# A hybrid decoder layer on one core: operand blocks fetched ahead, form sums on GpSimd, the norm chain in steps, and more Strassen units in FFN-out

## The chip, the cores and the metric

The kernel runs on one core of a Trainium2 chip. The core has TensorE (PE in the profile, its weight loads PEld), VectorE (DVE), ScalarE (ACT), GpSimd (POOL) and SyncE (SP, which only issues transfers); each takes its own instructions in order. The metric is the device time in microseconds of one execution, median of the runs.

## The reference

512 tokens, model width 2048, everything in float32. One layer:

```python
h = rmsnorm(x, attn_norm_g);  proj = h @ w_in        # u, v_sgu, q, k, v_att, g_a, g_b
y_a = u * chunked_spatial_gating(v_sgu);  y_b = stick_breaking_attention(q, k, v_att)
x = x + (sigmoid(g_a) * (y_a @ w_up_a) + sigmoid(g_b) * (y_b @ w_up_b)) @ w_o
h = rmsnorm(x, ffn_norm_g);  gate, up = split(h @ w_ffn_in)    # 2048 -> 2 x 5632
x = x + (silu(gate) * up) @ w_ffn_out                          # 5632 -> 2048
x = x + sigmoid(rmsnorm(x, ple_norm_g) @ w_ple_gate) * (p @ w_ple)
```

## The kernel before

Every product of float32 values is made of three matmuls (`mm3`): each operand is split into a high part (ScalarE's copy, L245 for activations and L313 for weights) and a low part (VectorE's subtraction, L246 and L310), and high x high, high x low and low x high are added up in PSUM. Activations lie transposed, 128 rows by 512 tokens.

The work is cut into **units**: 256 rows of the inner dimension against 256 columns of the output (an output **pair**). A unit is either plain ("P": four blocks of the weight, 12 matmuls of 512 columns) or one level of Strassen's scheme ("S": seven products of 128x128 blocks with half of the tokens, 21 matmuls of 256 columns; in FFN-in, where both output halves are doubled, L589 and L591). `OUT`, `PASSES` and `GATE` at the file's head say which unit of a stage is which. FFN-out has 22 units; their operands don't fit on the chip together, so it runs in three passes over the eight output pairs, of 8, 7 and 7 units, and the running sum goes to memory and back between passes (`sum`; pass 3 also reads `x1` and writes `x2`). The first pair of a stage (`j == 0`) is always computed plain.

An activation's operand is a **form**. Forms lie in the arena `parts`, 16 places (`PLACE`); a Strassen form takes two places of 1792 columns, a plain one 2048 columns. Raw blocks, weight landings and temporaries lie in the arena `wholes`. A form of a Strassen unit is built in steps: load the block (`load`, SP), scale by the norm's gain (`gained`, L451, where there is one), four sums of 128x256 (`plain_first`, L464, VectorE) and the split of the four plain blocks; a step later the split of three sums (128x3x256); last, once the plain pair has used it, the split of one more (128x256). `late_form` builds it for `x1` (FFN-in), `hid` (FFN-out) and `x2` (the gate), `x_form` for the input.

What sets the order: `tick()` is called two or more times in each double unit of a pair. A tick starts the first form of the queue `builds` if its source is there and the arenas have room, and runs the waiting steps of others. The schedule of each engine is then fixed when the program is built. Weights go through four landing blocks and three slots (`Weights`): SP brings a landing, and for a Strassen weight GpSimd issues a transfer that adds two blocks onto it (L317); ScalarE and VectorE split it into a slot (L313, L310), VectorE makes two sums of it (L329). `prepare_early` and `prepare_late` do this ahead of TensorE.

At the start, three output pairs of `p @ w_ple` (`ple_pair`) run while the first `x` blocks come in, then three pairs of the first projection share the plain forms of x (`w_first`). Five more ple pairs (two halves of output each, copied out by L766) stand between the out projection and FFN-in. `Norm` adds up squares (L831, L835); its chain is a matmul with ones (L844), a mean, a power on GpSimd (L852), and a spread of the result over the rows (L817, L819).

Of the kernel before, what the change touches and what calls it, by code (L numbers as in the profile page):

```python
# [63 lines left out]
def hybrid_layer(  # L64
# [44 lines left out]
    class Arena:  # L109
        def __init__(self, name, n, dt):  # L110
            self.tile, self.dt = keep.tile([P, n], dt, name=name), dt
            self.holes = [(0, n)]

        def take(self, n, how="low"):

            spots = []
            for start, size in self.holes:
                end = start + size
                if how == "place":
                    start = -(-start // PLACE) * PLACE  # L120
                if end - start >= n:
                    spots.append((-end, end - n) if how == "high" else (start, start))
# [7 lines left out]
        def give(self, block):  # L130
            holes = sorted(self.holes + [(block.start, block.n)])
# [54 lines left out]
    def tick():  # L186

        clock[0] += 1
        last, units = traced()[-1], dict(newest)
        if builds and builds[0].ready() and fits(builds[0].sizes):  # L190
            builds.popleft().step()
        while waiting and waiting[0][0] <= clock[0]:
            heapq.heappop(waiting)[2]()
        for i in reversed(traced()):
            if i is last:
                break
            if i.engine in units:
                tc.add_manual_dep(
                    i, units[i.engine],
                    mybir.DependencyInfo(mybir.DependencyClass.NoSync,  # L200
                                         mybir.DependencyReason.DATA),
                    reason="in its place among the units")

    class Staged:


        def __init__(self, steps):
            self.steps, self.result, self.done, self.at = steps, None, False, 0

        def advance(self):  # L210
            self.at += 1
            try:
                next(self.steps)
            except StopIteration as e:
                self.result, self.done = e.value, True

        def step(self):
            if not self.done:
                self.advance()
                if not self.done:  # L220
                    after(1, self.step)

        def get(self):
# [172 lines left out]
    def plain_weights(src):  # L396
        slot, w = Weights(src.rearrange("p (b c) -> p b c", b=4), 1, "P").get()
        return slot, w

    class Form(Staged):  # L400


        def __init__(self, kind, steps, sizes, ready):
            super().__init__(steps(self))
            self.kind, self.sizes, self.ready = kind, sizes, ready
            self.blocks, self.at_plain, self.used = None, kind == "P", False

        def get(self):
# [4 lines left out]
        def plain(self):  # L413

            if self.kind == "P":
                return self.get()
            while not self.at_plain:
                self.advance()
            return self.halves(self.operand())

# [9 lines left out]
        def use_plain(self):  # L430

            self.used = True
            if not self.done:
                after(1, self.step)

# [9 lines left out]
    def load(src, n=1024):  # L445
        b = take(n)
        nc.sync.dma_start(out=b.f(0, 1024), in_=src)
        return b
# [6 lines left out]
    def plain_first(form, raw):  # L455


        b, s, v = cut(raw.f()), take(768), take(256)
        t, x = cut(s.f()), form.operand()
        for out, p, q, op in ((t[:, 0], b[:, 1], b[:, 0], ALU.subtract),  # L460
                              (v.f(), b[:, 1], b[:, 3], ALU.subtract),
                              (t[:, 1], t[:, 0], b[:, 3], ALU.subtract),
                              (t[:, 2], t[:, 1], b[:, 2], ALU.add)):
            nc.vector.tensor_tensor(out=out, in0=p, in1=q, op=op)  # L464
# [12 lines left out]
    def late_form(src, ready=always, gain=None):  # L477


        def steps(form):  # L480
            w = src()
            form.blocks = (parts.take(2 * PLACE, "place"),)
            if gain:
# [5 lines left out]
        return Form("S", steps, [(parts, 2 * PLACE, "place")] + [(wholes, 1024, "low")] * 2, ready)  # L489

# [21 lines left out]

    def plain_form(src, ready=always, gain=None, raw=1024, how="low"):
        def steps(form):
            w = src()
            hi, lo = form.blocks = parts.take(1024, how), parts.take(1024, how)
            if gain:
                gained(hi.own(), w.f(), *gain)
# [7 lines left out]
            else:  # L526
# [5 lines left out]
        return Form("P", steps, [(parts, 1024, how)] * 2 + [(wholes, raw, "low")] * bool(raw),  # L532
                    ready)

# [212 lines left out]
    def ple_operands():  # L747
        raw = load(pT)
        hi, lo = parts.take(1024, "high"), parts.take(1024, "high")
        split_into(hi.own(), lo.own(), raw.f())  # L750
        give(raw)
        ps_p.extend((hi, lo))

    def ple_pair(j, planned=True):
        slot, ((wh, wl),) = next_weights() if planned else plain_weights(w_ple[j])
        if planned:
            prepare_early()
            prepare_late()
        o = wide()
        for i in range(2):  # L760
            ps = bank()
            for k in range(2):
                s = 2 * i + k
                xh, xl = (x.own(k * T, (k + 1) * T) for x in ps_p)
                mm3(ps, wh[:, s], wl[:, s], xh, xl, k == 0, k == 1)
            nc.scalar.activation(o[:, i * T : (i + 1) * T], ps, AF.Copy)  # L766
        d = tc.dram_tile([P, 1024], F32, name=nm("ple"))
# [13 lines left out]
    def load_x():  # L781
        x_raw.append(take(1024))
        nc.sync.dma_start(out=x_raw[-1].f(), in_=xT[len(x_raw) - 1])

    ple_operands()
    ple_pair(0, False)
    load_x()
# [36 lines left out]
    class Norm:  # L824
# [4 lines left out]
        def add(self, raw):  # L829
# [8 lines left out]
            if self.done == KU:  # L838
                self.chain = Staged(self.steps())

        def steps(self):
# [24 lines left out]
    def x_form(k):  # L866
        def steps(form):
            while len(x_raw) < min(k + 2, KU):
                load_x()
            form.blocks = (parts.take(2 * PLACE, "place"),)  # L870
            w = take(1024)
            gained(w.f(), x_raw[k].f(), g_attn, k)
# [225 lines left out]
    def made():  # L1098
# [3 lines left out]
        for i in range(1, 3):  # L1102
            ple_pair(i, False)
        ple_done()
        ps = [Pair("P" * KU) for _ in range(3)]
        for k in range(KU):
            for p, src in zip(ps, (w_first[i] for i in range(3))):
                slot, (w,) = plain_weights(src[:, k * 4 * P : (k + 1) * 4 * P])
                p.add("P", [w], [xs[k].plain()], False)
# [35 lines left out]
    def y_form(c, i):  # L1145
        return plain_form((lambda: y_a[i]) if c == "a" else lambda: load(y_spill[i]),
                          lambda: len(y_done) == 8, raw=0 if c == "a" else 1024)

# [70 lines left out]
    def spilled_form(kind, n, j, gain=None):  # L1219
        return (late_form if kind == "S" else plain_form)(  # L1220
            lambda: load(spill[n, j]), lambda: (n, j) in there, gain)

# [20 lines left out]
    ple_done()  # L1243
    after(3, norm2.chain.step)

# [29 lines left out]
    for c, kinds in enumerate(PASSES):  # L1275
# [4 lines left out]
        for j in range(KU):  # L1280
# [17 lines left out]
            give(before)  # L1298
    norm3.chain.step()

# [116 lines left out]
```

## Time and profile before

| | |
|---|---|
| runs, us | 2727.55 median, 2724.98 to 2731.51 (3) |
| profiled execution | 2727.38 us, span 2725.7 us, mean granted TensorE clock 0.996 |
| instructions | 45769, of them 17243 matmuls |
| busy | PE 99%, PEld 90%, DVE 76%, ACT 50%, POOL 16% |
| data moved | 529.05 MB, mean 194 GB/s |

Busy times of PE are those of pipelined matmuls, which overlap; the distance between the starts of two neighbours is what one costs. "<-" behind an idle time names the instruction that ended the wait. The stages by time: start and first projection to 92 us, the rest of the first projection with attention and gating to 800, the up projections to 1010, the out projection to about 1181 with the ple pairs behind it, FFN-in from 1227 to 2070, FFN-out's passes from 2070, 2243 and 2393, the gate from 2544 to the end (the last three a few microseconds either way, since neighbours overlap).

### The profile page before, as it was taken

What the parts mean: (1) busy time and instruction counts of PE and PEld (TensorE: products, weight loads), DVE (VectorE), ACT (ScalarE), POOL (GpSimd) and SP (SyncE); (2) the same over time, 40 slices, a digit from 0 to 9 for tenths busy, and PEclk for the clock granted to TensorE, in tenths of its full rate; (3) what the DMA queues carried; (4) which work ended last, traced back from release to release, by engine and by line L of the source; (5) the groups of instructions that cost most, each with busy time, mean ns of one, the idle gap of its engine ahead of it and who ended that gap; (6) DMA issues with size and microseconds to landing.
All of it is one profiled execution on the core that took longest, in us unless ns stands there. A gap on an engine that the chain in (4) does not pass through costs nothing.

```text
span 2725.7 us, 45769 instructions
## 1 busy us (share of the span) xinstructions
PE 2691.7 (99%) x17243; PEld 2442.4 (90%) x17243; DVE 2073.5 (76%) x3375; ACT 1353.6 (50%) x2043; POOL 444.3 (16%) x527
## 2 busy tenths in 40 slices
PE   8999999999999999999999999999999999999999
PEld 6899999999999889978888888888888998988898
DVE  7666767667777657668989898989898667778776
ACT  7655555555554334365444444444445344454543
POOL 0222223222220000001111111111111101111110
PEclk9999999999999999999999999999999999999999
DMA  7667676677776447767888878887887668788785
GB/s 220 157 175 172 174 177 170 166 174 191 172 193 207 135 138 203 199 206 200 210 205 199 209 201 206 203 202 204 204 199 211 178 179 237 197 251 237 224 222 156
DMA packets 302846, 529.05 MB, mean 194 GB/s; under 512 B 25632, under 2 KB 162848, under 8 KB 302624
## 3 DMA queue, kind: packets, MB, share of 16 engines
q1 hardware_dynamic: 241872, 425.70, 49.3%
q0 software_dynamic: 60752, 100.43, 23.6%
q8 instruction: 135, 2.21, 0.3%
q14 instruction: 87, 0.71, 0.1%
HBM read 478.84 MB, written 47.19 MB: 193 GB/s over the span
## 4 chain that ended last, share of the span: by engine, by line
PE 87%; DVE 5%; DMA 4%; ACT 2%; issue 1%; POOL 1%; SPq 0%; ACTq 0%; DVEq 0%; POOLq 0%
PE ps L251 18%; PE ps L252 18%; PE ps L250 18%; PE ps L589 17%; PE ps L591 9%; PE small L589 3%; DVE wlo L310 1%; PE small L591 1%; DMA wholes<-x 1%; DMA wholes<-w_ffn_out 1%; DVE parts L246 1%; DVE wholes L464 1%; PE small L1011 1%; PE small L987 1%; PE small L964 1%
## 5 line engine op out<-in xcount | busy, mean ns | idle before, releaser
L250 PE MATMUL ps<-parts,whi 128*128 128x256 f32 (+1 forms) x3995 | 1247.2, 314 | 19.4 <-ACT whi L313 10.8
L313 ACT ACTIVATE whi<-wholes 128x512 fp32r<-128x512 f32 (+4 forms) x950 | 855.6, 917 | 801.1 <-PE ps L251 330.5
L251 PE MATMUL ps<-parts,whi 128*128 128x256 f32 (+1 forms) x3960 | 1232.9, 311 | 3.0 <-DVE parts L246 3.0
L252 PE MATMUL ps<-parts,wlo 128*128 128x256 f32 (+1 forms) x3960 | 1231.1, 311 | 3.2 <-DVE wlo L310 3.0
L310 DVE TENSOR_TENSOR wlo<-wholes,whi 128x512 fp32r<-128x512 f32 (+4 forms) x950 | 964.4, 1048 | 147.1 <-ACT whi L313 145.8
L250 PEld LDWEIGHTS ps<-parts,whi 128*128 128x128 f32 x3995 | 763.9, 191 | 68.8 <-ACT whi L313 12.1
L251 PEld LDWEIGHTS ps<-parts,whi 128*128 128x128 f32 x3960 | 758.1, 191 | 49.0 <-DVE parts L246 6.2
L252 PEld LDWEIGHTS ps<-parts,wlo 128*128 128x128 f32 x3960 | 757.8, 191 | 42.9 <-DVE wlo L310 4.6
L589 PE MATMUL ps<-parts,whi 128*128 128x512 f32 x2064 | 725.3, 391 | 0.0
L591 PE MATMUL ps<-parts,wlo 128*128 128x256 f32 x2064 | 578.8, 280 | 0.0
L589 PEld LDWEIGHTS ps<-parts,whi 128*128 128x128 f32 x2064 | 386.7, 187 | 83.7
L591 PEld LDWEIGHTS ps<-parts,wlo 128*128 128x128 f32 x2064 | 390.3, 189 | 0.1
L329 DVE TENSOR_TENSOR wholes<-wholes 128x256 f32<-128x256 f32 (+1 forms) x794 | 328.0, 413 | 24.3 <-DMA wholes<-w_ffn_out 4.9
L317 POOL DMA_DIRECT2D wholes<-w_ffn_in x172 | 149.7, 871 | 746.2 <-DMA wholes<-w_ffn_in 246.0
L317 POOL DMA_DIRECT2D wholes<-w_in x132 | 118.7, 903 | 548.7 <-DMA wholes<-w_in 226.8
L649 DVE TENSOR_TENSOR out<-out,ps 128x256 f32<-128x256 f32 x258 | 107.3, 416 | 78.6 <-ACT out L646 78.6
L618 DVE TENSOR_TENSOR out<-out 128x256 f32<-128x256 f32 x59 | 25.0, 425 | 175.9 <-ACT out L615 175.6
L246 DVE TENSOR_TENSOR parts<-wholes,parts 128x1024 fp32r<-128x1024 f32 (+3 forms) x129 | 122.9, 963 | 23.5 <-ACT parts L245 23.3
L589 PE MATMUL small<-parts,whi 128*128 128x512 f32 x344 | 128.8, 391 | 0.0
L245 ACT ACTIVATE parts<-wholes 128x1024 fp32r<-128x1024 f32 (+3 forms) x129 | 105.8, 845 | 40.8 <-DMA wholes<-hid 16.9
L317 POOL DMA_DIRECT2D wholes<-w_ffn_out x56 | 57.0, 1034 | 404.7 <-DMA wholes<-w_ffn_out 181.2
L1256 ACT ACTIVATE out<-out 128x512 f32<-128x512 f32 x44 | 27.9, 633 | 167.0 <-DVE out L1255 167.0
(119 smaller groups left out, 1659.1 us busy)
## 6 DMA issues: line engine op xcount, KB each, us to landing
wholes<-w_ffn_in SPq DMA_DIRECT2D x172, 384.0 KB, 5.5
wholes<-w_in SPq DMA_DIRECT2D x132, 384.0 KB, 4.8
wholes<-w_ffn_in SPq DMA_DIRECT2D x172, 256.0 KB, 4.7
wholes<-w_ffn_in POOLq DMA_DIRECT2D x172, 256.0 KB, 5.3
wholes<-w_in SPq DMA_DIRECT2D x132, 256.0 KB, 4.0
wholes<-w_in POOLq DMA_DIRECT2D x132, 256.0 KB, 4.7
wholes<-x SPq DMA_DIRECT2D x32, 512.0 KB, 5.3
wholes<-w_ffn_out SPq DMA_DIRECT2D x31, 512.0 KB, 4.0
```

The source lines that it names most:

```text
L245: return (nc.scalar.activation(hi, src, AF.Copy), nc.vector.tensor_tensor(out=lo, in0=src, in1=hi.bitcast(F32), op=ALU.subtract))
L246: nc.vector.tensor_tensor(out=lo, in0=src, in1=hi.bitcast(F32), op=ALU.subtract))
L250: nc.tensor.matmul(ps[:, s], sh, mh[:, s], start=start, stop=False)
L251: nc.tensor.matmul(ps, sh, ml, start=False, stop=False)
L252: return nc.tensor.matmul(ps, sl, mh, start=False, stop=stop)
L310: in_turn(nc.vector.tensor_tensor(out=self.lo[:, blocks], in0=r, in1=h.bitcast(F32), op=ALU.subtract))
L313: in_turn(nc.scalar.activation(h, r, AF.Copy))
L317: nc.gpsimd.dma_start(out=raw[:, 3:5], in_=self.src[:, 1:3], accum_op=ALU.add)
L329: in_turn(nc.vector.tensor_tensor(out=o, in0=x, in1=y, op=ALU.add))
L589: nc.tensor.matmul(ps, wh[:, w], t[:, x].rearrange("p s c -> p (s c)"), start=first, stop=False)
L591: mark(nc.tensor.matmul(ps[:, :256], wl[:, w], t[:, x, 0], start=False, stop=last))
L649: in_turn(nc.vector.tensor_tensor(out=out, in0=x, in1=y, op=op))
```

## The change

1. `PASSES`: pass 1 has eight Strassen units, pass 2 seven, pass 3 five and two plain ones.
2. Forms whose block comes from memory (`far`) are fetched before they are built: in each tick one of the first three of `builds` (`AHEAD`) may issue its load, and it is built two ticks (`WAIT`) later at the earliest. Loads take the stretch of `wholes` that was given back longest ago (`"old"`).
3. `plain_first` puts the split of the plain blocks first and its four sums on GpSimd.
4. The norm chain starts by itself when the last block is added and goes on a step in each tick, with three ticks between the power and the spread; the explicit steps behind FFN-in's ple pairs and behind pass 3 are gone.
5. `pT` is loaded and split in two halves, behind the first ple weights; a ple pair runs its inner dimension outermost, over both banks.

```diff
-PASSES = "SSSSSPPP", "SSSSSPP", "SSSPPPP"
+PASSES = "SSSSSSSS", "SSSSSSS", "SSSSSPP"
+AHEAD, WAIT = 3, 2
...
+                    if how == "high":
+                        spots.append((-end, end - n))
+                    elif how != "old":
+                        spots.append((start, start))
+                    else:
+                        spots.extend((self.given[a // P : -(-(a + n) // P)].max(), a)
+                                     for a in {*range(start, end - n + 1, 256), end - n})
...
-        if builds and builds[0].ready() and fits(builds[0].sizes):
+        for f in list(builds)[:AHEAD]:
+            if not f.there and f.ready() and fits([(wholes, 1024, "old"), (wholes, 1024, "low")]):
+                f.fetch()
+                break
+        if builds and builds[0].ready() and builds[0].arrived() and fits(builds[0].sizes):
             builds.popleft().step()
...
+        def go_on(self):
+            if not self.going:
+                self.going = True
+                after(1, self.step)
...
+        def fetch(self):
+            self.block, self.there, self.due = self.src(), True, clock[0] + WAIT
+            self.sizes = self.sizes[:-1]
+        def arrived(self):
+            return self.there and clock[0] >= self.due
...
     def plain_first(form, raw):
-        b, s, v = cut(raw.f()), take(768), take(256)
+        b, s, v = cut(raw.f()), take(768, "old"), take(256, "old")
         t, x = cut(s.f()), form.operand()
+        split_into(x[:, 0:4, 0], x[:, 0:4, 1], b)
         for out, p, q, op in ((t[:, 0], b[:, 1], b[:, 0], ALU.subtract),
...
-            nc.vector.tensor_tensor(out=out, in0=p, in1=q, op=op)
-        split_into(x[:, 0:4, 0], x[:, 0:4, 1], b)
+            nc.gpsimd.tensor_tensor(out=out, in0=p, in1=q, op=op)
...
     def ple_operands():
-        raw = load(pT)
...
+        for k in (0, T):
+            nc.sync.dma_start(out=raw.f(k, k + T), in_=pT[:, k : k + T])
+            split_into(*(x.own(k, k + T) for x in ps_p), raw.f(k, k + T))
...
-        for i in range(2):
-            ps = bank()
-            for k in range(2):
+        banks = bank(), bank()
+        for k in range(2):
+            xh, xl = (x.own(k * T, (k + 1) * T) for x in ps_p)
+            for i, ps in enumerate(banks):
                 s = 2 * i + k
-                xh, xl = (x.own(k * T, (k + 1) * T) for x in ps_p)
                 mm3(ps, wh[:, s], wl[:, s], xh, xl, k == 0, k == 1)
...
             if self.done == KU:
                 self.chain = Staged(self.steps())
+                self.chain.go_on()
...
             nc.gpsimd.tensor_tensor(out=self.cols, in0=self.mean, in1=expo[:, :NT], op=ALU.pow)
-            yield
+            for _ in range(3):
+                yield
...
-    after(3, norm2.chain.step)
...
-    norm3.chain.step()
```

How the instructions stand now. First the queue of SP at the program's start (`xT` are the blocks of x, `w_first` and `w_in` the first projection's weights, `ple` stores of finished ple pairs), before:

```order
L293 DMA wholes<-w_first 128x512
L783 DMA wholes<-xT 128x1024 x2
L293 DMA wholes<-w_first 128x512 x3
L768 DMA ple_107<-out_88 128x1024
L293 DMA wholes<-w_first 128x512
L295 DMA wholes<-w_in 128x2x256
L768 DMA ple_148<-out_131 128x1024
L768 DMA ple_170<-out_153 128x1024
L295 DMA wholes<-w_in 128x2x256 x3
L783 DMA wholes<-xT 128x1024
L293 DMA wholes<-w_first 128x512 x2
```

and now:

```order
L819 DMA wholes<-xT 128x1024
L314 DMA wholes<-w_ple 128x512 x2
L314 DMA wholes<-w_first 128x512
L819 DMA wholes<-xT 128x1024 x2
L804 DMA ple_110<-out_91 128x1024
L804 DMA ple_151<-out_134 128x1024
L314 DMA wholes<-w_first 128x512 x2
L804 DMA ple_173<-out_156 128x1024
L819 DMA wholes<-xT 128x1024 x2
L316 DMA wholes<-w_in 128x2x256
```

Blocks 3 and 4 of x have moved ahead of the `w_in` transfers, of which four stood ahead of block 2 before.

Then ScalarE where pass 1 of FFN-out goes over into pass 2 (`whi` are high parts of weights, `parts` forms of `hid`, 4x256 their plain blocks and 3x256 their sums), before:

```order
L245 ACTIVATE parts<-wholes 128x4x256
L313 ACTIVATE whi_80<-wholes 128x1024
L615 ACTIVATE out_21017<-ps_20913 128x512
L245 ACTIVATE parts<-wholes 128x4x256
L313 ACTIVATE whi_78<-wholes 128x1024
L245 ACTIVATE parts<-wholes 128x3x256
L245 ACTIVATE parts<-wholes 128x4x256
L313 ACTIVATE whi_76<-wholes 128x1024
```

and now:

```order
L266 ACTIVATE parts<-wholes 128x4x256
L334 ACTIVATE whi_80<-wholes 128x1024
L266 ACTIVATE parts<-wholes 128x4x256
L266 ACTIVATE parts<-wholes 128x3x256
L266 ACTIVATE parts<-wholes 128x4x256
L266 ACTIVATE parts<-wholes 128x3x256
L334 ACTIVATE whi_78<-wholes 128x1024
L649 ACTIVATE out_21292<-ps_21122 128x512
```

The split of two forms' sums now stands ahead of the second plain weight (`whi_78`), where one of them came behind it before.

Last, GpSimd at the same place, now (`w_ffn_out` are the transfers that add onto a landing); before, only such transfers stood there:

```order
L338 DMA wholes<-w_ffn_out 128x512 x22
L497 TENSOR_TENSOR wholes<-wholes 128x256 x4
L338 DMA wholes<-w_ffn_out 128x512
L497 TENSOR_TENSOR wholes<-wholes 128x256 x3
L338 DMA wholes<-w_ffn_out 128x512
L497 TENSOR_TENSOR wholes<-wholes 128x256 x10
```

The 28 sums of pass 2's seven forms have come in between the transfers.

More of the change, by code (lines that the diff above doesn't have):

```diff
@@ L130, in give @@
         def give(self, block):
+            self.turns += 1
+            self.given[block.start // P : -(-(block.start + block.n) // P)] = self.turns
             holes = sorted(self.holes + [(block.start, block.n)])
@@ L406, in __init__, with raw @@
             self.blocks, self.at_plain, self.used = None, kind == "P", False
+            self.src, self.there, self.block, self.due = src, not far, None, 0
+        def fetch(self):
[3 more added lines that the diff above has]
+            return self.there and clock[0] >= self.due
+        def raw(self):
+            return self.src() if self.block is None else self.block
         def get(self):
@@ L432, in use_plain @@
             self.used = True
-            if not self.done:
-                after(1, self.step)
+            self.go_on()
         def free(self):
@@ L445, in load @@
     def load(src, n=1024):
-        b = take(n)
+        b = take(n, "old")
         nc.sync.dma_start(out=b.f(0, 1024), in_=src)
@@ L487, in steps @@
             return form.operand()
-        return Form("S", steps, [(parts, 2 * PLACE, "place")] + [(wholes, 1024, "low")] * 2, ready)
+        return Form("S", steps, [(parts, 2 * PLACE, "place")] + [(wholes, 1024, "low")] * 2, ready,
+                    src, far)
     def strassen_form(src, ready=always, gain=None, raw=PLACE):
@@ L747, in ple_operands, with ple_pair @@
     def ple_operands():
-        raw = load(pT)
-        hi, lo = parts.take(1024, "high"), parts.take(1024, "high")
-        split_into(hi.own(), lo.own(), raw.f())
+        raw = take(1024, "old")
+        ps_p.extend(parts.take(1024, "high") for _ in range(2))
+        for k in (0, T):
+            nc.sync.dma_start(out=raw.f(k, k + T), in_=pT[:, k : k + T])
+            split_into(*(x.own(k, k + T) for x in ps_p), raw.f(k, k + T))
         give(raw)
[L752 to L756, printed above, removed]
+    def ple_pair(j, weights=None):
+        slot, ((wh, wl),) = weights.get() if weights else next_weights()
+        if not weights:
             prepare_early()
```

39 lines of the change are left out of this document (21 added, 18 removed).

## The prediction

> **What bounds it.** I read the page's busy times first, then what TensorE waited for, then busy time by stage. The profiled execution took 2727.38 us around a span of 2725.7; the median of the three runs, 2727.55, lies 0.17 above it, so sums against 2727.4 stand for both. About 0.2%, 5.5 us, is what a measurement of this kernel can tell from no change.
>
> ```profile
> PE   2691.7 (99%) x17243; PEld 2442.4 (90%) x17243; DVE 2073.5 (76%) x3375; ACT 1353.6 (50%) x2043; POOL 444.3 (16%) x527
> ...
> PE ps L250 <- ACT whi L313: 10.8, 4, 6.3
> PE ps L250 <- ACT parts L245: 5.1, 4, 2.5
> PE ps L252 <- DVE wlo L310: 3.0, 4, 1.0
> PE ps L251 <- DVE parts L246: 3.0, 5, 0.8
> PE ps L250 <- ACT out L766: 2.9, 2, 1.7
> ...
> PE small L819 <- DVE diag L817: 1.1, 2, 0.8
> ```
>
> TensorE is busy 99%: the time is its instruction stream, plus some 34 us of idling in a few waits (total, times, longest). The next view says where: window, then busy times, granted clock, DMA share, GB/s.
>
> ```profile
> 0.00:45.00 45.00, 34.61 (x130) 27.08 (x131) 27.70 (x50) 31.04 (x45) 4.67 (x11) 0.92 0.83 255
> 1202.00:1230.00 28.00, 23.51 (x101) 18.66 (x102) 17.29 (x28) 19.02 (x29) 4.65 (x6) 0.97 0.93 283
> 1230.00:2040.00 810.00, 810.00 (x4667) 714.88 (x4666) 721.56 (x1296) 392.43 (x549) 144.40 (x166) 1.00 0.82 203
> 2082.00:2118.00 36.00, 33.75 (x189) 29.19 (x190) 27.73 (x44) 16.61 (x25) 6.02 (x6) 0.95 0.79 223
> 2260.00:2300.00 40.00, 36.95 (x259) 34.12 (x259) 29.57 (x52) 15.75 (x26) 4.78 (x5) 1.00 0.82 229
> 2300.00:2384.00 84.00, 84.00 (x606) 79.69 (x606) 60.64 (x100) 35.56 (x48) 11.53 (x11) 1.00 0.75 202
> 2384.00:2420.00 36.00, 35.93 (x204) 31.33 (x203) 28.38 (x41) 19.98 (x27) 4.24 (x4) 1.00 0.88 275
> 2420.00:2556.00 136.00, 133.99 (x774) 117.91 (x773) 112.25 (x159) 60.67 (x80) 14.56 (x14) 1.00 0.78 231
> 2556.00:2592.00 36.00, 33.06 (x193) 28.83 (x194) 27.17 (x48) 21.27 (x29) 4.14 (x4) 0.95 0.78 221
> ```
>
> Inside a stage nothing idles: FFN-in runs 810.00 of 810 us with VectorE at 89%. TensorE loses time only where a new set of forms is built: at the start (10.39 us, 6.3 of it before the first matmul), at FFN-in's start (4.49), at the three passes (2.25, 3.05, 0.07), in pass 3 (2.01) and at the gate (2.94): 14.8 us at boundaries. Where it idled, the granted clock fell as well (0.92, 0.97, 0.95, 0.95): another 3.6 us at the start and 0.8 + 1.8 + 1.8 = 4.4 at boundaries.
>
> **FFN-out's units.** A plain unit is 12 matmuls of 512 columns per output pair, a Strassen unit 21 of 256. The first and last of a run of 17 and of a run of 105, in pass 2:
>
> ```profile
> 2371.49 0.40 PE L251 MATMUL ps<-parts,whi 128*128 128x512 f32 x1
> ...
> 2375.14 0.39 PE L252 MATMUL ps<-parts,wlo 128*128 128x512 f32 x1
> 2375.37 0.28 PE L250 MATMUL ps<-parts,whi 128*128 128x256 f32 x1
> ...
> 2387.84 0.28 PE L252 MATMUL ps<-parts,wlo 128*128 128x256 f32 x1
> ```
>
> 3.65/16 = 0.228 us and 12.47/104 = 0.120 us from start to start (durations overlap). A plain unit costs 2.74, a Strassen one 2.52: 0.22 less. Strassen units go from 13 to 20 of 22, in the seven output pairs that are not computed plain: 7 x 7 = 49 conversions, 10.7 us. Fourteen pairs cease to be mixed and no longer open a bank in two halves (2 x 0.120 - 0.228 = 0.012 each), 0.2. **Term: -10.9.**
>
> What covers the rest of a Strassen unit, by these groups:
>
> ```profile
> L310 DVE TENSOR_TENSOR wlo<-wholes,whi 128x1280 fp32r<-128x1280 f32 x369 | 549.8, 1490 | 89.3 <-ACT whi L313 88.3
> L329 DVE TENSOR_TENSOR wholes<-wholes 128x256 f32<-128x256 f32 x738 | 312.0, 423 | 23.7 <-DMA wholes<-w_ffn_out 4.9 <-issue 1.4 <-DVE wlo L310 1.0
> L310 DVE TENSOR_TENSOR wlo<-wholes,whi 128x512 fp32r<-128x512 f32 x431 | 296.6, 688 | 31.4 <-ACT whi L313 31.1
> ...
> q1 hardware_dynamic: 241872, 425.70, 49.3%
> q0 software_dynamic: 60752, 100.43, 23.6%
> ...
> wholes<-w_ffn_in SPq DMA_DIRECT2D x172, 384.0 KB, 5.5
> wholes<-w_ffn_in SPq DMA_DIRECT2D x172, 256.0 KB, 4.7
> wholes<-w_ffn_in POOLq DMA_DIRECT2D x172, 256.0 KB, 5.3
> wholes<-w_ffn_out SPq DMA_DIRECT2D x31, 512.0 KB, 4.0
> ```
>
> VectorE: a double Strassen weight is 1.49 + 0.69 + 2 x 0.42 = 3.0 us in 5.04 of TensorE. Seven units make 10.6 us; combining and adding the running sum (2 x 0.69, 3 x 0.42 and about 1.2) makes it 14.4 of 17.6, 82%, below the 89% at which FFN-in lost nothing: cost 0.
> DMA: 1 MB costs all 16 engines 0.493 x 2725.7/425.70 = 3.16 us on q1 and 6.41 on q0. A Strassen double moves 0.655 MB and 0.262 MB, 3.75 us in 5.04; a plain one 0.524 MB, 1.66 in 5.47; a running sum or x1 block of 0.524 MB 1.66. Pass 2 before: 2.5 x 3.75 + 1.66 + 2 x 1.66 = 14.4 of 18.1 us, 0.79 (the row above has 0.75; FFN-in comes out at 0.81 for 0.82). After: pass 1 0.82, pass 2 3.5 x 3.75 + 3.3 = 16.4 of 17.6, **0.93**, pass 3 0.89. Pass 2 lies above every stretch that ran without idling (0.88 for 36 us), though below 1. Bounds: 0, or, if 0.88 is the limit, 1.0 us in each of seven pairs, 7 us. I take 0: four landing blocks keep the weights ahead, and 0.93 is not 1.
>
> **Start.** x block 3 is issued late, lands late, and TensorE stands:
>
> ```profile
> 25.97 0.38 SPq L783 DMA_DIRECT2D wholes<-xT  x1
> 34.61 1.33 ACT L451 ACTIVATE wholes<-wholes,gcol 128x512 f32<-128x512 f32 x2 [2.80 <-DMA wholes<-xT]
> 38.41 0.79 PE L250 MATMUL ps<-parts,whi 128*128 128x512 f32 x1 [3.58 <-ACT whi L313]
> ```
>
> In the new order on SP blocks 3 and 4 stand before the w_in transfers, behind the third ple store, and the landing no longer takes the block freed last. At stake are 10.39 - 6.3 = 4.1 us and 3.6 of clock. What is late next is the DMA supply (share 0.83): I take 5 of 7.7. pT comes in two halves behind the first weights, so the first matmul needs 512 columns instead of 1024: -1 (0 to -2). The norm chain is advanced by ticks: of the 1.1 us before L819, -0.8; its power now stands on POOL behind twelve sums, hidden since the chain starts two x blocks before its row is read. **Term: -7** (0 to -10).
>
> **Boundaries.** ScalarE takes its queue in order; before, a form's load stood in the same tick as the copy that reads it:
>
> ```profile
> ACT wholes L451 <- DMA wholes<-x: 19.1, 8, 4.0
> ...
> ACT parts L245 <- DMA wholes<-hid: 16.9, 10, 3.6
> ```
>
> Fetched two ticks ahead (5 us and more against 4 to 5.5 us of landing) these 36 us go. In their place the three-block split on ScalarE waits for four sums that leave VectorE (136, plus 28 for 7 new forms) and now queue on POOL among the accumulating transfers' issues:
>
> ```profile
> L464 DVE TENSOR_TENSOR wholes<-wholes x136: 411/418/426, 20.7 to 2558.7; 128x256 f32<-128x256 f32 x136
> L997 POOL COPY wholes<-wholes x24: 289/397/1427, 117.2 to 611.2; 128x128 f32<-128x128 f32 x24
> L1002 POOL TENSOR_SCALAR_AFFINE_SELECT wholes<-wholes 128x128 f32<-128x128 f32 x32 | 29.0, 906 | 0.4
> L310 DVE TENSOR_TENSOR wlo<-wholes,whi 128x512 fp32r<-128x512 f32 x1 | 0.8, 773 | 0.0
> ```
>
> No row has such a sum on POOL. Twice the columns of a copy: 2 x 0.289 = 0.58 at the least, 2 x 0.906 = 1.81 from the dearest row. I take 1.1, near twice the copies' middle (0.397) with some waiting: 4.4 us a form, where VectorE took 1.7. A copy ranged from 0.289 to 1.427: the long ones began under a wide split of VectorE, and the next 512-column split (last row) took 0.773 instead of 0.688, so VectorE loses about 0.09 per 128 columns read. Two inputs of 256 read four times that: 0.36 a sum. So VectorE gains 4 x (0.42 - 0.36) = 0.2 us a form: next to nothing.
> The Trainium skill (SBUF — State Buffer, "Who interferes with whom") says that a VectorE instruction with two SBUF inputs and a GpSimd one that reads SBUF exclude each other for the whole instruction; by that rule rival (e) comes about. The trace bears out that POOL waits for all of a split, not that VectorE waits for all of POOL. The same skill (GPSIMD Engine Reference, "When to use GPSIMD") puts a two-input addition at about twice VectorE's time; by that a sum would be an estimated 0.84 us.
> Does ScalarE's queue keep up? In the new order the plain split of form k+2 stands behind the sums of form k. Places come free from 5 us into a pass's last pair; sums begin near 6.5 and end at 6.5 + 4.4k, the split takes 1 more; TensorE wants plain form k+2 at 20.1 + 2.74(k+1). For k = 5: 29.5 against 36.5. It holds up to 5.8 us a form, 1.45 a sum. Pass 1 now fills all 16 places, so nothing of pass 2 is built early, as before at FFN-in's end. Of 14.8 + 4.4 us I take 5 off (bounds: all 19.2 off, or 8 more). **Term: -5.**
>
> **Sum.** 2727.4 - 10.9 - 7 - 5 = 2704.5; I say 2705.
>
> **Rivals.**
> (a) Only the stream shortens: waits on DMA turn into waits on POOL's sums of the same size. 2727.4 - 10.9 = 2716.5, with 6 us either way. For it: VectorE gains next to nothing. 20%.
> (b) Pass 2 is held by its transfers at 0.88: 7 us on the forecast, 2712; on (a), 2723. Against it: 0.93 stood for 28 us at FFN-in's start, where however TensorE idled. 8%.
> (c) Slower: a sum takes 1.81 us, 7.25 a form; the split of form 7 comes 5 x (7.25 - 5.8) = 7 us late at each of five boundaries and nothing is won there: 2727.4 - 10.9 - 7 + 36 = 2745. It decides from 1.45 us a sum, and turns the sign where it costs over 4 us a boundary. 6%.
> (d) All waits named vanish: 2727.4 - 10.9 - 10 - 19 = 2687, likelier about 2691. 8%.
> (e) VectorE stands for all 1.1 us of a sum instead of 0.36. In the 40 us at pass 2's start it was busy 29.6; without its own sums (5 forms x 1.7) and with POOL's (7 x 4.4) that is 51.9, 12 too many, of which two prepared weights (10 us) hide most. 3 us at five boundaries and nothing won there: 2727.4 - 10.9 - 7 + 15 = 2724.5, within 0.2%. Against it: the 0.773 row. 2%.
> The forecast's own range, 2696 to 2713, has 56%. (d) lies below 2694; what of (a), (b), (c) and (e) lies above 2721 is about 12%: the range is 2694 to 2721. Faster (under 2722): 56 + 8 (d) + 16 (a) + 5 (b) = 85%; within: 4 (a) + 2 (b) + 2 (e) = 8%; slower: 6 (c) + 1 (b) = 7%.
>
> **What the profile after would show.** Rows of 256 columns up by 1001, of 512 down by 574, both steps as above; pass 2's windows at full TensorE and a share near 0.93; the first matmul near 5.3 us and no wait near 38; no ScalarE waits on x or hid, but some on POOL's sums, at 0.8 to 1.2 us each. Wrong would be: sums over 1.45 us, TensorE idling inside pass 2, or new half-clock spells at the gate, which has the norm chain and eight forms to build at once.

## The result, and the profile after

The changed kernel takes 2763.22 us (median of 4 runs, 2750.89 to 2764.7) against 2727.86 for the one before in the same comparison: 1.0112 times as long, 95% interval 1.0092 to 1.0131. The forecast was 2705, its range 2694 to 2721; it is slower instead. The profiled execution took 2762.3 us around a span of 2760.6.

The page's first part (busy time, share, instructions) and what engines waited for (total, times, longest), after:

```profile
PE 2707.4 (98%) x17670; PEld 2461.3 (89%) x17670; DVE 2143.0 (78%) x3304; ACT 1377.5 (50%) x2066; POOL 641.1 (23%) x712
...
L497 POOL TENSOR_TENSOR wholes<-wholes 128x256 f32<-128x256 f32 x164 | 175.6, 1108 | 148.1 <-ACT wholes L483 79.4
```

```profile
ACT parts L266 <- POOL wholes L497: 36.0, 18, 7.9
...
PE ps L272 <- DVE parts L267: 21.0, 8, 5.3
...
ACT wholes L483 <- DMA wholes<-x: 12.7, 4, 4.1
...
PE ps L273 <- DVE wlo L331: 10.1, 11, 1.8
...
PE ps L271 <- ACT parts L266: 7.6, 4, 4.9
...
ACT parts L266 <- DMA wholes<-hid: 2.8, 1, 2.8
```

The 427 more matmuls are the forecast's 1001 more of 256 columns and 574 fewer of 512. ScalarE's waits for `hid` and `x` shrank from 16.9 and 19.1 us to 2.8 and 12.7, as meant, and 36.0 us of waiting for GpSimd's sums took their place. The new thing stands in TensorE's rows: what it waits for now is mostly VectorE (the low halves of forms, L267, and of weights, L331: 31.1 us, where the same two rows, L246 and L310, had 6.0 before). VectorE does none of the sums any more (136 before) and is busy 69.5 us longer than before.

By stage (window, busy times, granted clock, DMA share):

```profile
0.00:45.00 45.00, 35.83 (x135) 26.81 (x136) 33.28 (x37) 35.23 (x52) 23.24 (x31) 0.96 0.82 258
1202.00:1240.00 38.00, 34.00 (x138) 26.82 (x139) 25.64 (x33) 24.46 (x37) 17.79 (x18) 0.91 0.87 266
2092.00:2140.00 48.00, 37.89 (x183) 31.44 (x182) 44.59 (x46) 21.28 (x31) 30.20 (x31) 0.89 0.65 178
2276.00:2300.00 24.00, 18.72 (x79) 14.96 (x78) 20.98 (x25) 11.43 (x17) 14.56 (x16) 0.86 0.72 215
2300.00:2410.00 110.00, 110.00 (x919) 110.00 (x918) 91.16 (x140) 48.24 (x64) 33.37 (x33) 1.00 0.89 242
2580.00:2605.00 25.00, 17.84 (x78) 14.18 (x77) 20.21 (x29) 11.22 (x17) 8.53 (x9) 0.80 0.80 236
```

Pass 2 inside (fifth row) is full. The boundaries are worse than before, in idle time (10.1 us in the 48 at pass 1) and in the clock that follows it down (0.80 to 0.91). At the gate three spells of half the clock stand, of 3.4 us each, where before had one. Where TensorE stands at pass 2's start, the other engines read (start, duration, instruction):

```profile
2277.82 10.17 POOL L497 TENSOR_TENSOR wholes<-wholes 128x256 f32<-128x256 f32 x10 [1.40 <-DVE parts L267]
```

```profile
2282.35 0.85 ACT L266 ACTIVATE parts<-wholes 128x768 fp32r<-128x768 f32 x1 [7.88 <-POOL wholes L497]
```

```profile
2286.47 0.94 DVE L267 TENSOR_TENSOR parts<-wholes,parts 128x256 fp32r<-128x256 f32 x1
2287.33 0.94 DVE L350 TENSOR_TENSOR wholes<-wholes 128x256 f32<-128x256 f32 x1
2288.19 2.84 DVE L267 TENSOR_TENSOR parts<-wholes,parts 128x256 fp32r<-128x256 f32 x2
```

Ten sums in a row take 10 us, and ScalarE stands 7.9 us for them. VectorE's operations of 0.42 us take 0.94 beside them, and the first of the two in the last row takes 1.71 (the second, 1024 columns wide, its usual 1.21). TensorE waited 5.3 us behind the last row.

Where the time went, by the starts of the same instructions in the profiled executions (us; e11 and e5 are explained below and differ from each other in the sums alone):

| from, to | before | after | e1 | e5 | e11 |
|---|---|---|---|---|---|
| start to first transposition | 100.0 | 101.9 | 93.9 | 93.8 | 100.8 |
| to the first x1 store | 945.8 | 947.9 | 948.7 | 949.0 | 948.7 |
| to FFN-in's last matmul | 1024.3 | 1042.8 | 1023.1 | 1024.4 | 1036.5 |
| to the last x2 store (FFN-out) | 484.8 | 493.3 | 473.2 | 476.6 | 495.7 |
| to the end | 170.8 | 174.7 | 172.1 | 171.9 | 174.0 |

One row holds something that no boundary explains. FFN-in's interior, where nothing waits:

```profile
1450.00:2050.00 600.00, 600.00 (x3464) 529.74 (x3463) 534.45 (x959) 288.24 (x402) 107.03 (x123) 1.00 0.82 204
```

```profile
1450.00:2050.00 600.00, 600.00 (x3399) 520.30 (x3398) 523.38 (x938) 283.64 (x395) 107.63 (x122) 1.00 0.81 201
```

First before, then after: the same instructions at full granted clock, but 3464 matmuls in 600 us and then 3399. A pair of a 512- and a 256-column matmul takes 346.4 ns before and 353.0 after.

### The profile page after: what moved, and what is told of

Its sections match the earlier page's. It is cut to its first block, busy times and chain, and to the rows that moved or that the text cites. A ratio compares the mean times of both kernels' runs of the same rounds, so it can differ in the third digit from the quotient of the medians.

```text
span 2760.6 us, 46886 instructions
## 1 busy us (share of the span) xinstructions
PE 2707.4 (98%) x17670; PEld 2461.3 (89%) x17670; DVE 2143.0 (78%) x3304; ACT 1377.5 (50%) x2066; POOL 641.1 (23%) x712
## 4 chain that ended last, share of the span: by engine, by line
PE 89%; DVE 5%; issue 2%; DMA 2%; POOL 1%; ACT 1%; SPq 0%; DVEq 0%; ACTq 0%; POOLq 0%
PE ps L273 19%; PE ps L272 19%; PE ps L271 18%; PE ps L623 17%; PE ps L625 9%; PE small L623 3%; DVE wlo L331 2%; DVE parts L267 1%; PE small L625 1%; POOL wholes L497 1%; DMA wholes<-x 1%; PE small L1050 1%; PE small L1003 1%; PE small L942 1%; PE small L1026 1%
## 5 line engine op out<-in xcount | busy, mean ns | idle before, releaser
L271 PE MATMUL ps<-parts,whi 128*128 128x256 f32 (+1 forms) x4128 | 1270.8, 309 | 9.1 <-ACT parts L266 7.6
L272 PE MATMUL ps<-parts,whi 128*128 128x256 f32 (+1 forms) x4107 | 1256.7, 306 | 21.0 <-DVE parts L267 21.0
L334 ACT ACTIVATE whi<-wholes 128x512 fp32r<-128x512 f32 (+4 forms) x957 | 872.4, 928 | 791.2 <-PE ps L272 294.3
L273 PE MATMUL ps<-parts,wlo 128*128 128x256 f32 (+1 forms) x4107 | 1255.6, 306 | 10.1 <-DVE wlo L331 10.1
L331 DVE TENSOR_TENSOR wlo<-wholes,whi 128x512 fp32r<-128x512 f32 (+4 forms) x957 | 1003.0, 1084 | 160.3 <-ACT whi L334 159.1
L272 PEld LDWEIGHTS ps<-parts,whi 128*128 128x128 f32 x4107 | 789.1, 192 | 61.0 <-DVE parts L267 25.0
L271 PEld LDWEIGHTS ps<-parts,whi 128*128 128x128 f32 x4128 | 793.0, 192 | 50.5 <-ACT parts L266 9.4
L273 PEld LDWEIGHTS ps<-parts,wlo 128*128 128x128 f32 x4107 | 788.9, 192 | 45.6 <-DVE wlo L331 14.5
L623 PEld LDWEIGHTS ps<-parts,whi 128*128 128x128 f32 x2064 | 387.7, 188 | 97.8 <-issue 2.2
L625 PEld LDWEIGHTS ps<-parts,wlo 128*128 128x128 f32 x2064 | 389.7, 189 | 0.0
L350 DVE TENSOR_TENSOR wholes<-wholes 128x256 f32<-128x256 f32 (+1 forms) x836 | 355.2, 425 | 25.1 <-DMA wholes<-w_ffn_in 4.9
L497 POOL TENSOR_TENSOR wholes<-wholes 128x256 f32<-128x256 f32 x164 | 175.6, 1108 | 148.1 <-ACT wholes L483 79.4
L267 DVE TENSOR_TENSOR parts<-wholes,parts 128x768 fp32r<-128x768 f32 (+4 forms) x145 | 156.7, 1098 | 27.9 <-ACT parts L266 27.9
L266 ACT ACTIVATE parts<-wholes 128x768 fp32r<-128x768 f32 (+4 forms) x145 | 113.0, 813 | 52.5 <-POOL wholes L497 36.0
```

The lines of the kernel that those rows point to most:

```text
L266: return (nc.scalar.activation(hi, src, AF.Copy), nc.vector.tensor_tensor(out=lo, in0=src, in1=hi.bitcast(F32), op=ALU.subtract))
L267: nc.vector.tensor_tensor(out=lo, in0=src, in1=hi.bitcast(F32), op=ALU.subtract))
L271: nc.tensor.matmul(ps[:, s], sh, mh[:, s], start=start, stop=False)
L272: nc.tensor.matmul(ps, sh, ml, start=False, stop=False)
L273: return nc.tensor.matmul(ps, sl, mh, start=False, stop=stop)
L331: in_turn(nc.vector.tensor_tensor(out=self.lo[:, blocks], in0=r, in1=h.bitcast(F32), op=ALU.subtract))
```

## The experiments

Theory 1: a two-input operation on GpSimd stops VectorE's beside it, and that is the loss. Theory 2: the Strassen passes are what is late. Beside both: why FFN-in's pairs became longer.

**e1: the sums back on VectorE, all else as changed.**

```diff
-            nc.gpsimd.tensor_tensor(out=out, in0=p, in1=q, op=op)
+            nc.vector.tensor_tensor(out=out, in0=p, in1=q, op=op)
```

> The changed kernel with its 164 sums back on VectorE (0.424 us each, 69.5 us in all), everything else as changed. Theory 1 (the sums on GpSimd cost the time: a POOL sum stretches the VectorE operation beside it by about 0.54 us, 71.1 us in all, against 69.5 us that left VectorE, and a form's four sums in series take 4.4 us instead of 1.7): the PE stalls at the stage boundaries (49 us listed) fall to about 25, FFN-in keeps 19.41 us per m, time 2705 to 2722. Theory 2 (the passes of Strassen units alone are what is late: 14 S forms instead of 10 in passes 1 and 2 to make at the boundaries): stalls at 2105, 2112, 2131, 2291 and 2435 stay, 2735 to 2760. By either, if FFN-in's 19.79 us per m comes of where the blocks lie, it stays, which is 13 us; if it comes of a late evacuation beside a POOL sum, it goes back to 19.41.

2725.94 us (2712.68 to 2728.85, 10 runs), 0.9976 of before (0.9956 to 0.9995): 37 us less than after, though 4 above the range of theory 1. The profiled run is the fastest, 2712.68, and the other nine lie at 2723.67 and above. In that run TensorE's two waits on VectorE are back at 6.1 us (31.1 in after), and FFN-in runs at 346.5 ns a pair:

```profile
PE ps L273 <- DVE wlo L331: 3.6, 3, 1.9
...
PE ps L272 <- DVE parts L267: 2.5, 3, 1.0
```

```profile
1450.00:2050.00 600.00, 600.00 (x3463) 528.98 (x3462) 534.40 (x958) 288.58 (x402) 106.41 (x122) 1.00 0.83 203
```

So the sums on GpSimd are the loss; by which way, e8 and e9 tell. ScalarE's waiting alone doesn't tell it: in e1 ScalarE waits 25.5 us for the same sums on VectorE (36.0 for GpSimd's in after). The blocks' places, which are as in after, don't set the pairs' rate.

**e2: before, with only the sums on GpSimd**, behind the first split.

```diff
+        split_into(x[:, 0:4, 0], x[:, 0:4, 1], b)
...
-            nc.vector.tensor_tensor(out=out, in0=p, in1=q, op=op)
-        split_into(x[:, 0:4, 0], x[:, 0:4, 1], b)
+            nc.gpsimd.tensor_tensor(out=out, in0=p, in1=q, op=op)
```

> The kernel before with only the four sums of a form moved to GpSimd, behind the first split. Theory 1 (sums on GpSimd cost the time): slower by 10 to 35 us, 2738 to 2763, with PE waits on VectorE's splits at the start (28 to 62 us), at the x1 stage (1202 to 1240) and at the passes' boundaries. Theory 2 (the passes are what is late): within 5 us of 2728.

2784.19 us, 1.0190 (1.0161 to 1.0220): 56 us, more than the range said. The profiled run, 2773.17, has FFN-in at 346.4 ns a pair from 1337 us on, as before has, and lies 46 us above before's profiled run; the other three runs lie 10 to 13 us higher still. So the sums alone make this kernel slower too.

**e3: before, with only the new units.**

```diff
-PASSES = "SSSSSPPP", "SSSSSPP", "SSSPPPP"
+PASSES = "SSSSSSSS", "SSSSSSS", "SSSSSPP"
```

> The kernel before with only the new units in FFN-out (15 Strassen units, then five and two plain ones). Theory 1 (sums on GpSimd cost the time; the shorter stream is real): the stream is 10.9 us shorter, more S forms to make with VectorE at the boundaries take back up to 5: 2715 to 2724. Theory 2 (the passes are what is late): 2735 to 2755. A third (pass 2's transfers hold PE, 3.75 us of 16 engines in each 5.04 us): PE idle inside pass 2 and not only at its start, 2725 to 2735.

2740.85 us, 1.0050 (1.0032 to 1.0067), so theory 2 has a part of the truth: by themselves the units cost 13 us (8.7 in the profiled run). FFN-out takes 491.5 us there, 6.7 more than before although its stream is 10.9 shorter, and the gate 4.8 more. The third guess falls; the waits are at the boundaries, for forms and for blocks of `hid` (before: 5.1, 3.0 and 16.9):

```profile
ACT parts L245 <- DMA wholes<-hid: 22.4, 12, 6.1
...
PE ps L250 <- ACT parts L245: 13.3, 7, 4.2
...
PE ps L251 <- DVE parts L246: 6.9, 6, 3.0
```

**e4: after, without fetching ahead.**

```diff
-AHEAD, WAIT = 3, 2
+AHEAD, WAIT = 0, 2
...
-            self.src, self.there, self.block, self.due = src, not far, None, 0
+            self.src, self.there, self.block, self.due = src, True, None, 0
```

> The changed kernel with no block fetched ahead of its form (sums on GpSimd, new units and the norm's steps as changed). Theory 1: the sums still cost what they cost and a load's landing is waited for besides (19 us of ScalarE waits on blocks of x before): 2760 to 2785. If fetching ahead itself is the harm (blocks held longer, forms begun later): 2730 to 2750.

2766.26 us (2755.45 to 2776.9), 1.0133 (1.0097 to 1.0169): not to be told from after. While GpSimd's sums stand, fetching ahead buys nothing measurable.

**e5: e1, with FFN-in's matmuls in the order 512, 512, 256, 256.**

```diff
+                if self.doubled:
+                    ps = self.at(i)
+                    for u, ((wh, wl), t) in enumerate(zip(ws, xs)):
+                        nc.tensor.matmul(ps, wh[:, w], t[:, x].rearrange("p s c -> p (s c)"),
+                                         start=start and u == 0, stop=False)
+                    for u, ((wh, wl), t) in enumerate(zip(ws, xs)):
+                        mark(nc.tensor.matmul(ps[:, :256], wl[:, w], t[:, x, 0], start=False,
+                                              stop=stop and u == n - 1))
```

(and the loop that alternates them is left to the other stages).

> The kernel of e1 (changed, sums on VectorE) with FFN-in's matmuls in another order: of each product the 512-column matmuls of both units first, then both 256-column ones, instead of 512, 256, 512, 256. Theory of the rhythm (TensorE runs a 512 and a 256 in 346.7 ns or in 353.3 ns, the same instructions without a wait, and which of the two it is was set by the last wait before it; the runs 13 us apart are these two): no pairs of 353 ns, all runs at 2711 to 2717 with a scatter under 6 us. Rival (the 13 us between runs arise somewhere else, at the boundaries): median 2724 to 2729 as e1, scatter as there.

2716.75 us (2710.96 to 2719.41, 5 runs), 0.9960 (0.9947 to 0.9973): 11 us below before. The spread, 8.5 us, is half of e1's but over the 6 expected; why two of the five runs lie near 2711 is open. The pairs:

```profile
1450.00:2050.00 600.00, 600.00 (x3442) 523.47 (x3442) 530.80 (x951) 286.27 (x400) 106.13 (x122) 1.00 0.82 202
```

348.6 ns, between the two rates seen so far, 346.4 and 353.0, called the quick and the slow rhythm from here on. This version beats both kernels.

**e6: e1, with the units of before.**

```diff
-PASSES = "SSSSSSSS", "SSSSSSS", "SSSSSPP"
+PASSES = "SSSSSPPP", "SSSSSPP", "SSSPPPP"
```

> The kernel of e1 with the units of before in FFN-out (five Strassen and three plain, five and two, three and four). If the new units save their stream of 10.9 us as soon as blocks are fetched ahead, FFN-out (last FFN-in matmul to the last x2 store) is 484 us against 473 in e1, and the time 2722 to 2726 where FFN-in runs at 346.7 ns a pair, 2734 to 2739 at 353.3. If the units are worth nothing and all of e1's gain is the fetching ahead: FFN-out 470 to 476, within 3 us of e1.

2730.07 us, 1.0011 (0.9997 to 1.0025), below the 2734 expected for the slow rhythm. FFN-out takes 482.0 us against e1's 473.2, near what was expected, but the gate 167.7 against 172.1: of the new units' 8.8 us the gate gives half back. The profiled run shows the slow rhythm with the sums on VectorE and the old units, so neither makes it:

```profile
1450.00:2050.00 600.00, 600.00 (x3398) 520.28 (x3397) 525.46 (x944) 283.78 (x394) 105.28 (x121) 1.00 0.81 199
```

**e8: e1, with four GpSimd additions per form besides, into a tile that nobody reads.**

```diff
+        for k in range(4):
+            nc.gpsimd.tensor_tensor(out=idle, in0=b[:, 1], in1=b[:, k], op=ALU.add)
```

> The kernel of e1 with four additions of 128x256 per form on GpSimd besides, into a tile that nobody reads, at the place where the changed kernel has its sums: the exclusion alone, with no form that waits for GpSimd. Theory of the exclusion (a two-input operation on GpSimd stops VectorE's beside it for about 0.54 us): VectorE's operations are stretched by 60 to 75 us in all, most of the sums' cost is back: 2742 to 2765. Theory of the latency (a form's sums take 4.4 us in series on GpSimd and the splits behind them come late; VectorE has room for the stretching): 2722 to 2735.

2793.02 us, 1.0248 (1.0231 to 1.0265): 67 us above e1, more than expected, with no form waiting for GpSimd. VectorE runs the same instructions in e1 (first row) and in e8:

```profile
PE 2679.7 (99%) x17670; PEld 2453.4 (91%) x17670; DVE 2127.2 (78%) x3468; ACT 1373.9 (51%) x2066; POOL 463.8 (17%) x548
```

```profile
PE 2712.9 (97%) x17670; PEld 2465.8 (88%) x17670; DVE 2195.4 (79%) x3468; ACT 1375.2 (49%) x2066; POOL 654.3 (23%) x712
```

It is 68.2 us longer: 0.42 us for each of 164 additions that it doesn't need, as long as a sum of its own. TensorE idles 46.5 us more than in e1, 28 of them behind the same two rows, and its mean granted clock is 0.989 against 0.997:

```profile
PE ps L273 <- DVE wlo L331: 24.8, 16, 4.0
...
PE ps L272 <- DVE parts L267: 9.7, 7, 2.2
```

The additions also hold the raw block and the transfers queued behind them on GpSimd a little longer; e9 has such holding too, without the second input.

**e9: after, with a one-input copy on GpSimd in the place of each sum.** The forms' sums are left out by this.

```diff
-            nc.gpsimd.tensor_tensor(out=out, in0=p, in1=q, op=op)
+            nc.gpsimd.tensor_copy(out=out, in_=p)
```

> The changed kernel with a GpSimd copy (one input) in the place of each GpSimd sum, so that the forms are not Strassen's: the chain on GpSimd stays, the two-input operation goes. Theory of the exclusion: VectorE is stretched by under 15 us instead of 71, the time falls to 2715 to 2738. Theory of the latency: with four copies of 0.5 to 0.7 us still in series behind the first split it stays at 2745 or above.

2721.94 us, 0.9971 (0.9958 to 0.9985): 41 us below after, and the profiled run has the slow rhythm as after has (353 ns from 1351 us on), so that isn't the difference. The chain on GpSimd is still there, 73% as long (0.809 against 1.108 us each), and ScalarE still waits 18.9 us behind it, but TensorE's two waits on VectorE are 4.7 us; VectorE's 3304 instructions take 51.4 us less than in after's first row:

```profile
PE 2691.7 (99%) x17670; PEld 2453.9 (90%) x17670; DVE 2091.6 (77%) x3304; ACT 1376.1 (51%) x2066; POOL 585.4 (22%) x712
...
L497 POOL COPY wholes<-wholes 128x256 f32<-128x256 f32 x164 | 126.5, 809 | 138.1 <-ACT wholes L483 81.4 <-DVE parts L267 26.9 <-DMA wholes<-hid 16.4
```

So the loss is that the two-input sums and VectorE's operations exclude each other, and the longer chain is at most a small part of it. e9 also bears on what the sums cost on VectorE: it has none there, and is only 1 to 4 us below e1 (by the ratios and by the medians), though the copies' own stretching of VectorE, 17 us in all, may hide some.

**e7: e5, without fetching ahead.**

```diff
-AHEAD, WAIT = 3, 2
+AHEAD, WAIT = 0, 2
...
-            self.src, self.there, self.block, self.due = src, not far, None, 0
+            self.src, self.there, self.block, self.due = src, True, None, 0
```

> The kernel of e5 (sums on VectorE, matmuls of FFN-in in the order 512, 512, 256, 256) with no block fetched ahead of its form: what fetching ahead is worth when the sums are on VectorE. If the gap between e3 (2741, new units without it) and e1 (2712 to 2727) is the fetching ahead: FFN-out 485 to 492 us against 473 to 477, ScalarE's and VectorE's splits at the passes' boundaries wait for blocks of hid again, 2728 to 2740. If it is the split ahead of the sums: within 4 us of e5 (2717).

2721.93 us, 0.9983 (0.9973 to 0.9992): fetching ahead is worth about 5 us, less than either range needed (2728 to 2740, or within 4 of e5). FFN-out takes 488.0 us against 476.6, as expected, and part of it comes back at the gate (169.4 against 171.9). ScalarE's wait for `hid` is 13.7 us, against 5.2 in e5.

**e10 and e11: before and after, with e5's order of matmuls** (its diff, on `before` and on the changed kernel).

> The kernel before with FFN-in's matmuls in the order 512, 512, 256, 256 and nothing else. Theory of the rhythm: most runs of before are at 346.7 ns a pair already, so the median moves by under 4 us (2722 to 2728), and no run lies 11 to 18 us above the others, as 4 of the 40 runs of before did. Rival (the order saves time in every pair): lower by 8 us and more.

2729.18 us (2726.2 to 2735.59), 1.0013 (1.0004 to 1.0023), 1 above the range. Before was at 346.4 ns already, so the order costs it 2.2 ns in each of 2408 pairs, 5 us; 2 were measured. The highest run lies 6 us above the median.

> The changed kernel, sums on GpSimd, with FFN-in's matmuls in the order 512, 512, 256, 256. Theory: the 13 us of the rhythm go and the exclusion's 36 us over e5 stay: 2746 to 2756, no pairs at 353 ns, FFN-in 19.4 to 19.5 us per m. Rival (FFN-in is slower beside GpSimd's sums or for where its blocks lie): 2758 to 2768 as before the order changed.

2754.86 us (2751.71 to 2757.43), 1.0106 (1.0090 to 1.0122): 8 us below after. The rhythm cost after 353.0/346.4 over the 690 us from 1403 to FFN-in's end, 13 us; the new order takes 4 of them again. The rest, 38 us over e5, is the sums alone: e5 and e11 differ in nothing else. The table's last columns, 40 apart, place it: start 7, the x1 stage with FFN-in's start 12, FFN-out 19, gate 2.

**e12: e5, with the sums ahead of the first split again.**

```diff
-        split_into(x[:, 0:4, 0], x[:, 0:4, 1], b)
         for out, p, q, op in ((t[:, 0], b[:, 1], b[:, 0], ALU.subtract),
...
             nc.vector.tensor_tensor(out=out, in0=p, in1=q, op=op)
+        split_into(x[:, 0:4, 0], x[:, 0:4, 1], b)
```

> The kernel of e5 with a form's sums ahead of its first split again, as in the kernel before. If the order matters (ScalarE starts the split at once when it comes first; VectorE's half of it otherwise waits 1.7 us behind the sums): 2 to 8 us more, 2719 to 2725. If not: within 2 us of e5.

2717.92 us, 0.9965 (0.9953 to 0.9978): 1.2 above e5, inside the spread. On VectorE the order of split and sums made no measurable difference.

## Why the prediction was wrong, point by point

The time came 58 us above the forecast. The changed kernel with its sums on VectorE and FFN-in at 346.5 ns (e1's profiled run) lies 14.7 us below before, where 22.9 were forecast; the sums on GpSimd add 38 (e11 against e5) and the slow rhythm 13.

- **Boundaries, -5: the step that failed.** The duration was right (1.1 us taken, 1.108 measured, the shortest 0.72), and so was the balance: a sum was to cost VectorE 0.36 us, it cost 71.1/164 = 0.43 (durations beside sums less those of the same shapes alone), and 69.5 us of sums left. "VectorE gains next to nothing" is what happened. But from a balance of zero the text went on to a cost of zero. On VectorE the sums seem to cost the kernel little (1 to 4 us, e9 against e1), which fits sums that stand in its gaps but doesn't show it; the stretching falls on whatever runs, at boundaries on the half of a form or weight that TensorE waits for (31.1 us there, 6.1 in e1). e8, where the sums stay on VectorE as well, prices such stretching: 68.2 us of it, 67 of time. Measured by e11 against e5, the sums cost 33 us behind the start, in a term that was to spare 5.
- **ScalarE's queue.** It was compared form by form with TensorE's demand, with sums beginning at 6.5 us and nothing in the way. In the trace the sums waited for VectorE's splits, VectorE's operations stretched beside the sums, and ScalarE stood 36.0 us. The loss is not read from this wait: ScalarE stood 25.5 us for the sums in e1 as well.
- **Start, -7.** The first matmul came at 4.9 us (5.3 forecast), the wait near 38 went, and with the sums on VectorE the start gains 6.1 us (e1; the unchanged start took 97.4 and 98.0 us in e3 and e10 against 100.0 in before, so 3.5 to 6.1). On GpSimd they take 8.0 of it back; the prediction put them only on the boundaries.
- **Stream, -10.9.** The counts and the steps were right, and pass 2 runs full at a share of 0.89 (0.93 forecast), so rival (b) falls. FFN-out shortened by 8.8 us only where the forms are in time (e6 against e1); without that (e3) the boundaries took 17.6 us, a cost that the sum did not have. Half of the 8.8 goes at the gate.
- **The rhythm, 13 us.** It stood in no term.
- **Signs of being wrong.** Of the three named, sums stayed under 1.45 us and TensorE didn't idle inside pass 2; half-clock spells at the gate did come. None of them looked at how long VectorE's operations take, where the loss arose.
- **Chances.** By the text's own split 15% lies above 2722, not about 12% above 2721.
- **Rivals.** (a) was right that waits on sums take the place of waits on loads, but the 36.0 us of new waits match its 36 by luck: 15.5 us of the waits on `x` and `hid` stayed. It left out that VectorE pays besides. (c) had the sign, by a sum of 1.81 us that didn't occur. (e) had the mechanism, at 2%: the row of 0.773 us was held against it, but that row stands beside a GpSimd operation with one input and says nothing of two. Its price, 3 us at each boundary, was too low as well, since it let prepared weights hide work that TensorE in fact waited for.

## What to carry to other kernels

In this kernel, work moved from VectorE to GpSimd that reads two operands from SBUF was not off VectorE: 0.43 us of stretching came back for each 0.42 us sum. It falls on the operation that happens to run, which at a boundary is the critical one. Price a move by who is delayed, not by the sum of busy times; a tile that nobody reads, as in e8, measures that in one run. And where runs of one kernel lie 13 us apart, count the instructions of a stretch without waits before explaining the difference by the edit.

## What the runs showed of the hardware

**VectorE and GpSimd.** Of the 90 VectorE operations that ran beside a single sum in after, 26 took 0.52 to 0.57 us longer than alone, 7 took 0.30 to 0.49 longer, 2 over 1.0, and 55 ran on as alone (within 0.015). Beside a single one-input copy (e9) those that were held took mostly 0.18 to 0.20 longer. Of the 18 VectorE operations with one input in PSUM that ran beside sums from end to end, none was over 0.002 us longer than alone. The Trainium skill (SBUF — State Buffer, "Who interferes with whom") says just that of a VectorE instruction with two inputs in SBUF against one with at most one; the trace agrees. The Trainium skill calls the port pair that the two engines share, in the same section, an exclusive lock and says that whoever issues first gets it for the whole instruction. The trace goes further, since here a VectorE operation that had started first was kept through three of four sums and ended during the fourth:

```profile
44.99 3.19 DVE L331 TENSOR_TENSOR wlo<-wholes,whi 128x512 fp32r<-128x512 f32 x1
45.15 3.63 POOL L497 TENSOR_TENSOR wholes<-wholes 128x256 f32<-128x256 f32 x4
...
48.23 0.50 PE L273 MATMUL ps<-parts,wlo 128*128 128x512 f32 x1 [0.48 <-DVE wlo L331]
```

A split of 0.69 us took 3.19, and TensorE waited for it. Four other operations in after were held beside four sums in the same way, for 2.3 to 2.7 us.

**Two rhythms of TensorE.** FFN-in's alternating 512- and 256-column matmuls run in 230 + 117 ns, or in a cycle of three pairs of 233 + 117, 241 + 120 and 236 + 113 ns (one pair 353), and stay in it for hundreds of microseconds without a wait. A wait can change it over. In after the last change came at 1403:

```profile
1399.81 1.01 POOL L497 TENSOR_TENSOR wholes<-wholes 128x256 f32<-128x256 f32 x1 [3.83 <-DMA wholes<-hid]
1400.13 0.97 DVE L683 TENSOR_TENSOR out<-out 128x256 f32<-128x256 f32 x1
...
1402.96 0.47 PE L623 MATMUL ps<-parts,whi 128*128 128x512 f32 x1 [0.18 <-DVE out L683]
```

A sum stretched a combination of outputs (0.97 for 0.42), a PSUM bank came free late, TensorE stood 0.18 us, and from there to FFN-in's end, 690 us, a pair took 353. That this wait made the change is read from its place in time. The traces of after, e2, e8 and e9 have ten such changes: eight right behind a wait of 0.03 to 1.08 us, two where a pair came 0.15 to 0.2 us late without a wait that the profile lists. Other waits, four of them in e4, changed nothing; which wait leads into which rhythm was not found out. The order 512, 512, 256, 256 showed one rhythm only, 348.6 ns, in all five profiles taken with it. That the runs 11 to 16 us apart (one run of after, nine of e1, a few of before) are the two rhythms fits the sizes and e5, but those runs left no trace.
